# One transformer block on one core: w_ada laid out with a feature in each row, one multiply-and-sum a block on VectorE, and the first columns in four rounds of 2, 3, 5 and 6 blocks

## The chip, the core and the metric

The program runs on one core of a Trainium2 chip. The metric is the device time of one execution, in microseconds (us), from the start of the launch to its end; lower is better. The core's engines run side by side, each through its own list of instructions in a fixed order: TensorE (PE) multiplies matrices into PSUM, VectorE (DVE) and ScalarE (ACT) work element by element, SyncE (SP) issues nearly all transfers from HBM to SBUF, and GpSimd (POOL) does little here.

## The reference

One block over 256 tokens of width D = 2048, all in float32. What matters here is cut out of it:

```python
c_act = jax.nn.silu(c)                                  # (1, 2048)
mod = c_act @ w_ada[l] + b_ada[l]                       # w_ada (2048, 6 * 2048)
sh1, sc1, gt1, sh2, sc2, gt2 = jnp.split(mod, 6, axis=-1)
h = ada_norm(x, g_norm1[l], sh1, sc1)                   # rmsnorm(x, g) * (1 + sc1) + sh1
aq, ak, av, iq, ik, iw, hq, hf, hi, hog, ga, gh = split_cols(h @ w_in[l])
...
x = x + gt1[:, None] * (merged @ w_out[l])
h2 = ada_norm(x, g_norm2[l], sh2, sc2)
x = x + gt2[:, None] * hier_moe(h2, ...)                # 32 experts
return rmsnorm(x, g_final)
```

`mod` is a product of one vector with a matrix of 2048 x 12288: 100.7 MB that are read once. Each column of `h @ w_in` needs all 2048 features of h, and so all of sh1 and sc1; sc2, sh2, gt1 and gt2 are needed only from the product with w_out on.

## The kernel before, in words

A block is 128 features (KT = 16 blocks make 2048). Every product of the dense part (w_in, w_attn_up, w_hgrn_up, w_out) is taken as three float32r products: ACT rounds a weight tile to its high part (`split_w`, line 254), DVE subtracts for the low part (line 255), and PE runs high x high, high x low, low x high (`three`, lines 276 to 278) for each of the two halves t of the tokens. A pair of weight blocks against 512 columns is thus one ACT instruction and one DVE instruction of 128x1024 and 12 matmuls.

Weights come through `unit` (line 206): a ring of four SBUF tiles of up to 1 MB, filled by SP in the program's order. A tile is loaded anew when the engine that reads it last is done with it.

**First columns.** While w_ada is still being read, `first_columns` already works on 9 chunks of w_in's columns (seven of 512, two of 292) in rounds over blocks of features. FIRST_GROUPS gives each round its first block and its number of blocks: (0, 2), (2, 2), (4, 4), (8, 4), (12, 4). A round needs sc1 and sh1 of its own blocks only. At its start h of these blocks is made (lines 510 to 524); then, chunk by chunk, the weights are split, multiplied, and the PSUM results copied out by ACT (first round) or added by DVE onto the sums so far (line 543, two adds a chunk). Behind each chunk stands a unit of w_ada for the next round (`ada_block`). From the fifth chunk of the last round on, steps of attention and of the recurrence are taken in between.

**The vector times w_ada.** In HBM w_ada is packed with input features as partitions. In the first rounds a unit is 1 MB and PE multiplies it by a zero-padded 128x32 tile of c (line 494); for sh1 of rounds 2 and 3 (FIRST_DVE, counted from 0) DVE does it instead, with one multiply-and-add of 128x512 for each input block (line 489). The partial sums lie over partitions or in rows, so `ada_columns` (line 398) turns them into columns with small PE products. The other 64 units (`next_ada`) are taken one behind each unit of a later product, with each sixth call left out: the first 8 by PE (line 422), the other 56 by DVE, four instructions of 128x512 each (line 427). The gates gt1 and gt2 stay as partial sums over the partitions, with the bias in one row, and `gate_rows` sums them with a matrix of ones.

**The rest.** `middle_columns` (names hcol, hog, gate), `merge` (up) and `project` (out) follow. Last come the 32 experts: 384 tiles of 1 MB of weights are loaded and multiplied, in an order written by hand. Outside the experts the order on each engine is set by a scheduler from the program's dependencies and its written order.

Of the kernel before, what the change touches and what calls it, by code (L numbers as in the profile page):

```python
# [29 lines left out]
FIRST_GROUPS = ((0, 2), (2, 2), (4, 4), (8, 4), (12, 4))  # L30
FIRST_DVE = (2, 3)
# [57 lines left out]

def _blocks():  # L90


    for j0, nk in FIRST_GROUPS:
        ku = KT // nk
        for q in range(nk):
            for part in (1, 0):
                yield "w_ada", ku * q, ku, part * D + 128 * j0, 128 * nk
        for c0, n in FIRST_COLS:
            yield "w_in", j0, nk, c0, n
    for c0 in range(2 * D, 6 * D, 512):  # L100
        for q in range(4):
            yield "w_ada", 4 * q, 4, c0, 512
# [18 lines left out]
def packed(arrays):  # L121
# [14 lines left out]
class Block:  # L136
# [27 lines left out]
    def t2(self, shape, dt=F32, tag="t2"):  # L164
        return self.dn.tile(shape, dt, name=self.name("t2"), tag=tag, bufs=25)
# [115 lines left out]
    def prepare(self):  # L281
# [5 lines left out]
        crow = self.dn.tile([16, 128], F32, name="crow")  # L287
        nc.sync.dma_start(crow, a["c"].rearrange("o (r f) -> (o r) f", f=128))
# [24 lines left out]
        ps = self.misc()  # L313
        nc.tensor.transpose(ps[:, :16], crow, self.ident[:16, :16])
        th = self.sm([128, 32])
        nc.scalar.activation(th[:, :16], ps[:, :16], AF.Tanh, scale=0.5)
        ca = self.keepd([128, 16])
        nc.vector.scalar_tensor_tensor(ca, th[:, :16], 1.0, ps[:, :16], op0=OP.add, op1=OP.mult)
        nc.vector.tensor_scalar(ca, ca, 0.5, None, op0=OP.mult)
        self.ca = ca  # L320
        self.mod = {n: self.keep([128, 16]) for n in ("sc2", "sh2")}
        self.gates_in = {}
        self.ada_i, self.ada_call, self.ada_acc = 0, 0, [None, None]
        cpad = self.keepd([128, 16, 32])
        nc.gpsimd.memset(cpad, 0.0)
        nc.vector.tensor_copy(cpad[:, :, 0], ca)
        self.cpad = cpad
# [65 lines left out]
    def ada_columns(self, part, rhs):  # L393

        n, m = rhs.shape[-1], part.shape[-1] // 128
        ps = self.misc()
        for i in range(m):
            self.nc.tensor.matmul(ps[:, n * i:n * i + n], part[:, i * 128:(i + 1) * 128], rhs, start=True, stop=True)
        return ps[:, 0:m * n].rearrange("p (i r) -> p i r", r=n)

    def next_ada(self):

        self.ada_call += 1
        if self.ada_i == 64 or self.ada_call % ADA_SKIP == 0:
# [7 lines left out]
        c0 = 128 * base + 512 * c
        w = self.unit(("w_ada", 4 * q, c0, 512))
        if b > 7 and q == 0 and b not in self.gates_in:
            self.gate_room(b)
        if q == 0:
            self.ada_acc[on_dve] = self.gates_in[b] if b > 7 else self.t2([128, 512]) if on_dve else self.adabank()
        acc = self.ada_acc[on_dve]
        for i in range(4):
            j = 4 * q + i  # L420
            if not on_dve:
                nc.tensor.matmul(acc[32 * i:32 * i + 32, :], self.cpad[:, j, :], w[:, i, :], start=q == 0, stop=q == 3,
                                 skip_group_check=True)
            elif j == 0 and b < 8:
                nc.vector.tensor_scalar(acc, w[:, i, :], self.ca[:, j:j + 1], None, op0=OP.mult)
            else:
                nc.vector.scalar_tensor_tensor(acc, w[:, i, :], self.ca[:, j:j + 1], acc, op0=OP.mult, op1=OP.add)
        if q == 1 and 7 < b + 1 < 16:
            self.gate_room(b + 1)
        if q == 3 and b < 8:  # L430
            if not on_dve:
                ps, acc = acc, self.t2([128, 512])
                nc.scalar.activation(acc, ps, AF.Copy)
            v = self.ada_columns(acc, self.ones[:, 0:1])[:, :, 0]
            f = slice(4 * c, 4 * c + 4)
            add = self.bsc[:, 16:32] if name == "sc2" else self.cols[:, base:base + 16]
            nc.vector.tensor_add(self.mod[name][:, f], v, add[:, f])

    def gate_room(self, b):

        t = self.t2([128, 512])
        self.nc.gpsimd.memset(t, 0.0)
        c0 = (32 * 128, 80 * 128)[b // 12] + 512 * (b % 4)
        self.nc.gpsimd.dma_start(t[0:1, :], self.a["b_ada"][:, c0:c0 + 512])
        self.gates_in[b] = t

    def gate_rows(self, b, out):

        ps = self.misc()
        self.nc.tensor.matmul(ps, self.ones, self.gates_in[b], start=True, stop=True)  # L450
        self.nc.scalar.activation(out, ps, AF.Copy)


    def first_columns(self):
# [11 lines left out]
        bank = {}  # L466
# [4 lines left out]
        def ada_block(g, u):  # L471

            if g > last:
                return
            j0, nk = groups[g]
            ku = 16 // nk
            if u == 0:
                bank[g] = self.adabank(), self.t2([128, 512]) if g in FIRST_DVE else None
            ps, acc = bank[g]
            q, b = divmod(u, 2)  # L480
            if q * ku >= KT:
                return
            c0 = (D, 0)[b] + 128 * j0
            w = self.unit(("w_ada", ku * q, c0, 128 * nk))
            for i in range(ku):
                j = ku * q + i
                if b and acc is not None:
                    if j:
                        nc.vector.scalar_tensor_tensor(acc, w[:, i, :], self.ca[:, j:j + 1], acc, op0=OP.mult, op1=OP.add)
                    else:  # L490
                        nc.vector.tensor_scalar(acc, w[:, i, :], self.ca[:, j:j + 1], None, op0=OP.mult)
                    continue
                r = 64 * b + 32 * (i % 2)
                nc.tensor.matmul(ps[r:r + 32, 0:128 * nk], self.cpad[:, j, :], w[:, i, :], start=j < 2, stop=j >= KT - 2,
                                 skip_group_check=True)

        for u in range(8):
            ada_block(0, u)
        self.first_norm()
        for g, (j0, nk) in enumerate(groups):  # L500
# [6 lines left out]
            ps, acc = bank[g]  # L507
            rows = 128 if acc is None else 64
            part = self.t2([128, 512])
            nc.scalar.activation(part[:rows, 0:128 * nk], ps[:rows, 0:128 * nk], AF.Copy)  # L510
            v = self.ada_columns(part[:rows, 0:128 * nk], self.half[:rows])
            w = v[:, :, 1:2] if acc is None else self.ada_columns(acc, self.ones[:, 0:1])
            f = slice(j0, j0 + nk)
            G = self.sm([128, nk, 2])
            nc.vector.tensor_add(G[:, :, 0], v[:, :, 0], self.bsc[:, f])
            nc.vector.tensor_mul(G[:, :, 0], G[:, :, 0], self.cols[:, 96 + j0:96 + j0 + nk])
            nc.vector.tensor_add(G[:, :, 1], w[:, :, 0], self.cols[:, f])
            for i in range(nk):
                j = j0 + i
                h = self.t1([128, 256])  # L520
# [909 lines left out]
```

## Time and profile before

| | us |
|---|---|
| median of 3 runs | 1835.61 (1833.42 to 1838.31) |
| the profiled execution | 1836.52 |
| its span, first to last instruction | 1834.8 |
| PE busy | 1713.7 (93%) |
| DVE busy | 903.0 (49%) |
| ACT busy | 505.5 (28%) |

PE's busy time counts matmuls with modelled ends, which overlap: a stretch in which PE is busy all the time is one in which it had work, and the distance from one matmul's start to the next tells what a matmul costs. The shares are averages over stages with different limits, so the stages are read apart.

### The profile page before, as it was taken

How to read it: one execution, taken by the hardware profiler on the slowest of the kernel's cores; microseconds unless marked ns; L12 is line 12 of the kernel's file. 1: busy time of each engine (PE TensorE's matmuls, PEld its weight loads, DVE VectorE, ACT ScalarE, POOL GpSimd, SP SyncE). 2: the span in 40 equal slices, each digit the busy share in tenths (PEclk: the TensorE clock that was granted, in tenths of full speed). 3: DMA queues.
4: the chain of work that ended last, by engine and by line, in shares of the span. 5: the costliest groups of instructions: out<-in, count | busy, mean ns of one | idle time of the engine just before them, and what ended most of it. 6: DMA issues, size and time to landing. Idle time of an engine off the chain costs nothing. (4 is left out here: it accounts for less than half of the span.)

```text
span 1834.8 us, 20408 instructions
## 1 busy us (share of the span) xinstructions
PE 1713.7 (93%) x7925; PEld 992.0 (54%) x7925; DVE 903.0 (49%) x1636; ACT 505.5 (28%) x845; POOL 17.2 (1%) x36
## 2 busy tenths in 40 slices
PE   7899999999999999997999998998989989989895
PEld 4566676677778877774443443433434434334232
DVE  3677479698778899974122321232123221222125
ACT  3333244555554433443220020110201102002003
POOL 0000000000000000000000000000000000000000
PEclk9999999999999999997999999999999999999997
DMA  7887745776668888976999999999999999999995
GB/s 284 292 286 282 288 158 205 250 293 250 230 232 327 335 310 318 348 261 265 379 422 421 421 421 422 421 421 421 421 422 421 421 421 422 421 421 421 422 377 192
DMA packets 96485, 630.39 MB, mean 344 GB/s; under 512 B 14864, under 2 KB 17216, under 8 KB 22016
## 3 DMA queue, kind: packets, MB, share of 16 engines
q1 hardware_dynamic: 95008, 626.01, 86.1%
q0 software_dynamic: 1200, 2.96, 0.6%
q8 instruction: 64, 1.05, 0.2%
q14 instruction: 37, 0.30, 0.0%
q10 hardware_dynamic: 176, 0.07, 0.0%
HBM read 626.90 MB, written 2.10 MB: 343 GB/s over the span
## 5 line engine op out<-in xcount | busy, mean ns | idle before, releaser
L1160 PE MATMUL moe_acc<-moe_u,moe_xg 128*64 128x512 f32 x2048 | 487.6, 600 | 42.1 <-DMA moe_u<-w_exp_up 42.1
L1160 PEld LDWEIGHTS moe_acc<-moe_u,moe_xg 128*64 128x64 f32 x2048 | 157.3, 137 | 319.1 <-issue 219.0
L1267 PE MATMUL moe_acc<-moe_u,moe_hT 128*64 128x512 f32 (+1 forms) x1040 | 242.1, 590 | 10.9 <-DMA moe_u<-w_exp_down 10.9
L1219 DVE COPY moe_gu<-moe_acc 128x512 f32<-128x512 f32 x32 | 22.1, 691 | 355.5 <-PE moe_acc L1160 355.5
L1267 PEld LDWEIGHTS moe_acc<-moe_u,moe_hT 128*64 128x64 f32 x1040 | 88.3, 137 | 145.9 <-issue 109.5
L1270 DVE SCALAR_TENSOR_TENSOR moe_ys<-moe_acc,moe_cw,out_t 128x512 f32<-128x512 f32 (+1 forms) x65 | 48.3, 742 | 180.7 <-PE moe_acc L1267 180.6
L1272 ACT ACTIVATE moe_yp<-moe_ys 128x512 fp32r<-128x512 f32 (+1 forms) x65 | 40.5, 623 | 310.4 <-DVE moe_ys L1270 310.4
L276 PE MATMUL gate_acc<-gate_wr,first_t 128*128 128x512 f32 x256 | 103.3, 404 | 0.0
L277 PE MATMUL gate_acc<-gate_wl,first_t 128*128 128x512 f32 x256 | 102.2, 399 | 0.0
L278 PE MATMUL gate_acc<-gate_wr,first_t 128*128 128x512 f32 x256 | 101.8, 398 | 0.0
L1352 DVE TENSOR_TENSOR out_t<-out_t,moe_ps 128x512 f32<-128x512 f32 (+1 forms) x130 | 82.0, 672 | 35.6 <-PE moe_ps L1351 35.6
L1341 ACT ACTIVATE moe_xg<-moe_ps,pre_c,pre_c 128x256 f32<-128x256 f32 (+1 forms) x144 | 70.5, 539 | 80.9 <-PE moe_ps L1338 79.9
L254 ACT ACTIVATE gate_wr<-gate_u 128x1024 fp32r<-128x1024 f32 x64 | 67.8, 1059 | 85.9 <-PE gate_acc L278 80.7
L1230 ACT ACTIVATE moe_si<-moe_ps 128x256 f32<-128x256 f32 x32 | 12.2, 381 | 280.4 <-PE moe_ps L1227 280.4
L255 DVE TENSOR_TENSOR gate_wl<-gate_u,gate_wr 128x1024 fp32r<-128x1024 f32 x64 | 78.0, 1222 | 23.0 <-ACT gate_wr L254 22.8
L1338 PE MATMUL moe_ps<-moe_P,out_t 128*128 128x256 f32 (+1 forms) x576 | 82.2, 292 | 3.5 <-ACT moe_Sw L1256 2.8
L1338 PEld LDWEIGHTS moe_ps<-moe_P,out_t 128*128 128x128 f32 x576 | 72.7, 194 | 22.0 <-issue 16.1
L276 PE MATMUL lb_acc<-lb_wr,first_t 128*128 128x512 f32 (+1 forms) x208 | 79.3, 386 | 3.2 <-ACT first_t L523 2.4
L277 PE MATMUL lb_acc<-lb_wl,first_t 128*128 128x512 f32 (+1 forms) x208 | 79.1, 380 | 2.7 <-DVE lb_wl L255 2.7
L1351 PE MATMUL moe_ps<-moe_yp,moe_S 128*128 128x512 f32 (+1 forms) x260 | 78.4, 422 | 2.6 <-ACT moe_yp L1272 2.3
L278 PE MATMUL lb_acc<-lb_wr,first_t 128*128 128x512 f32 (+1 forms) x208 | 78.4, 378 | 0.0
L1351 PEld LDWEIGHTS moe_ps<-moe_yp,moe_S 128*128 128x128 f32 x260 | 44.0, 189 | 60.3 <-issue 49.9
(436 smaller groups left out, 2507.1 us busy)
## 6 DMA issues: line engine op xcount, KB each, us to landing
moe_u<-w_exp_gate SPq DMA_DIRECT2D x128, 1024.0 KB, 19.8
moe_u<-w_exp_up SPq DMA_DIRECT2D x128, 1024.0 KB, 19.8
moe_u<-w_exp_down SPq DMA_DIRECT2D x126, 1024.0 KB, 19.8
gate_u<-w_in SPq DMA_DIRECT2D x32, 1024.0 KB, 4.9
gate_u<-w_ada SPq DMA_DIRECT2D x26, 1024.0 KB, 5.6
lb_u<-w_in SPq DMA_DIRECT2D x20, 1024.0 KB, 6.0
first_u<-w_ada SPq DMA_DIRECT2D x17, 1024.0 KB, 6.7
out_u<-w_out SPq DMA_DIRECT2D x16, 1024.0 KB, 7.6
```

The source lines that it names most:

```text
L254: nc.scalar.activation(hi, raw, AF.Copy)
L255: nc.vector.tensor_sub(lo, raw, hi.bitcast(F32))
L276: mm(out, lr, hi, start=start, stop=False)
L277: mm(out, lr, lo, start=False, stop=False)
L278: mm(out, ll, hi, start=False, stop=stop)
L1160: nc.tensor.matmul(gu[e][64 * k:64 * k + 64, :], xg[g][j][:, CAP * i:CAP * i + CAP], w[k][:, jj, :], start=j == 0, stop=j == KT - 1, skip_ ...
L1267: nc.tensor.matmul(yp[64 * i:64 * i + 64, :n], h[i][:, f, :], w[i][:, f, :], start=f == 0, stop=f == 3, skip_group_check=True)
L1270: nc.vector.scalar_tensor_tensor(raw, yp[:, :n], cw, self.gt2[:, c0:c0 + n], op0=OP.mult, op1=OP.mult)
L1338: nc.tensor.matmul(ps[:, 0:n], self.xs[t][i][:, j * 128:(j + 1) * 128], P[t], start=t == 0 and i == 0, stop=t == 1 and i == 1)
L1341: nc.scalar.activation(x, ps[:, 0:n], AF.Identity, scale=self.mod["sc2"][:, j:j + 1], bias=self.mod["sh2"][:, j:j + 1])
L1351: self.nc.tensor.matmul(ps[:, :n], sc[:, t * 128:(t + 1) * 128], ys[i], start=i == 0, stop=i == 1)
L1352: self.nc.vector.tensor_add(self.z[t][:, s], self.z[t][:, s], ps[:, :n])
```

## The change

- `w_ada` is transposed in HBM: a row is an output feature, with its 2048 inputs. A block of 128 features is one tile of 128x2048 (1 MB, as before). `ada` loads it and takes it by one VectorE instruction, `tensor_tensor_reduce`: multiply by c, broadcast over the partitions, and sum along the row into one column of `mod`.
- c is loaded broadcast to 128 partitions (128x2048) at the head of SP's queue, and silu is one ACT instruction.
- PE has no w_ada product any more, `ada_columns` and the gates' rows go; `gate_rows` makes four diagonal tiles on ACT and sums these with the matrix of ones.
- The first columns run in four rounds of 2, 3, 5 and 6 blocks. A round's w_in tiles have at most 4 blocks (`pieces`), so the rounds of 5 and 6 load two a chunk; an odd block is split by instructions of half the width. h of a round is made before the last chunk of the round ahead of it; the scaling of h moves from DVE to ACT.
- The 512-wide SBUF buffers are 22 instead of 25; PSUM has one more buffer for small results.

```diff
-FIRST_GROUPS = ((0, 2), (2, 2), (4, 4), (8, 4), (12, 4))
-FIRST_DVE = (2, 3)
+FIRST_GROUPS = ((0, 2), (2, 3), (5, 5), (10, 6))
...
+SH1, SC1, GT1, SH2, SC2, GT2 = range(6)
+ADA_ORDER = [(part, j) for part in (SC2, SH2, GT1, GT2) for j in range(KT)]
...
+def pieces(j0, nk):
+
+    n = -(-nk // 4)
+    for i in range(n):
+        a, b = nk * i // n, nk * (i + 1) // n
+        yield j0 + a, b - a
...
+    out["w_ada"] = np.ascontiguousarray(arrays["w_ada"][0].T)
...
-        nc.sync.dma_start(crow, a["c"].rearrange("o (r f) -> (o r) f", f=128))
+        self.ca = self.keepd([128, D])
+        nc.sync.dma_start(self.ca, a["c"].to_broadcast([128, D]))
...
+        nc.scalar.activation(self.ca, self.ca, AF.Silu)
...
+    def ada(self, part, j):
+
+        w = self.big.tile([128, D], F32, name=self.name("u"), tag="ring", bufs=4)
+        r = 128 * (KT * part + j)
+        self.nc.sync.dma_start(w, self.a["w_ada"][r:r + 128, :])
+        self.nc.vector.tensor_tensor_reduce(w, w, self.ca, 1.0, 0.0, OP.mult, OP.add, self.mod[part][:, j:j + 1])
+
+    def next_ada(self):
+
+        self.ada_call += 1
+        if self.ada_i < len(ADA_ORDER) and self.ada_call % ADA_SKIP:
+            self.ada(*ADA_ORDER[self.ada_i])
+            self.ada_i += 1
...
+        todo = [[(part, j) for j in range(j0, j0 + nk) for part in (SC1, SH1)] for j0, nk in groups] + [[]]
...
+            ahead = todo[g + 1]
             for c, (c0, n) in enumerate(cols):
+                if c == len(cols) - 1 and g < last:
+                    features(g + 1)
                 acc = [self.acc(), self.acc()]
-                raw = self.unit(("w_in", j0, c0, n))
...
+                for u0, m in pieces(j0, nk):
+                    raw = self.unit(("w_in", u0, c0, n))
+                    for q in range(0, m, 2):
+                        hi, lo = self.split_w(raw[:, q:min(q + 2, m), :], n)
...
-                for u in range(8):
-                    if min(u, len(cols) - 1) == c:
-                        ada_block(g + 1, u)
+                k = len(cols) - 1
+                for block in ahead[len(ahead) * c // k:len(ahead) * (c + 1) // k]:
+                    self.ada(*block)
```

The scheduler's order shows where the work stands now. First VectorE, in the second round of the first columns, before: `first_acc` and `first_t` are the sums of line 543, `first_u ... pre_d` a w_ada tile times c, `first_wl` the low part of a weight tile.

```order
L489 SCALAR_TENSOR_TENSOR first_t_550<-first_u_579,pre_d_91,first_t_550 128x512 x2
L255 TENSOR_TENSOR first_wl_590<-first_u_587,first_wr_589 128x1024
L543 TENSOR_TENSOR first_t_277<-first_t_277,first_acc_527 128x512
L543 TENSOR_TENSOR first_t_279<-first_t_279,first_acc_528 128x512
L489 SCALAR_TENSOR_TENSOR first_t_550<-first_u_579,pre_d_91,first_t_550 128x512
```

The same engine and round in the changed kernel; the multiply-and-sum (`ISA`, line 382) has a second row of 128x1 that writes out its sum.

```order
L382 ISA first_u_531,pre_d_88<-first_u_531,pre_d_69 128x2048
L382 ISA pre_d_88 128x1
L471 TENSOR_TENSOR first_t_262<-first_t_262,first_acc_499 128x512
L471 TENSOR_TENSOR first_t_264<-first_t_264,first_acc_500 128x512
L251 TENSOR_TENSOR first_wl_539<-first_u_536,first_wr_538 128x1024
L251 TENSOR_TENSOR first_wl_555<-first_u_536,first_wr_554 128x512
L382 ISA first_u_566,pre_d_89<-first_u_566,pre_d_69 128x2048
L382 ISA pre_d_89 128x1
```

Every w_ada tile of the round now stands in VectorE's list, between the splits and the adds that PE waits for, and a split of three blocks takes two instructions.

PE in the second round before, between two chunks of columns: `first_ada` is the product of a w_ada tile with the padded c.

```order
L277 MATMUL first_acc_586<-first_wl_590,first_t_106 128x512
L278 MATMUL first_acc_586<-first_wr_589,first_t_108 128x512
L494 MATMUL first_ada_549<-first_u_607,pre_d_96 32x512 x4
L276 MATMUL first_acc_613<-first_wr_617,first_t_106 128x292
L277 MATMUL first_acc_613<-first_wl_618,first_t_106 128x292
```

PE between two chunks of the same round in the changed kernel:

```order
L273 MATMUL first_acc_500<-first_wl_520,first_t_101 128x512
L274 MATMUL first_acc_500<-first_wr_519,first_t_103 128x512
L272 MATMUL first_acc_534<-first_wr_538,first_t_101 128x512
L272 MATMUL first_acc_535<-first_wr_538,first_t_101 128x512
L273 MATMUL first_acc_534<-first_wl_539,first_t_101 128x512
```

The w_ada products are gone from PE's list; nothing takes their place.

## Rows read from the trace of the kernel before

**Rows 1.** The page: span, and busy time of PE.
```profile
span 1834.8 us, 20408 instructions
PE 1713.7 (93%) x7925; PEld 992.0 (54%) x7925; DVE 903.0 (49%) x1636; ACT 505.5 (28%) x845; POOL 17.2 (1%) x36
```

**Rows 2.** Windows by stage: length, engines' busy time, PE clock, DMA share, GB/s.
```profile
0.00:32.00 32.00, 19.10 (x148) 13.19 (x148) 11.82 (x42) 8.54 (x20) 2.65 (x8) 1.00 0.83 311
32.00:66.00 34.00, 31.98 (x168) 21.95 (x168) 13.48 (x19) 19.08 (x31) 0.00 (x0) 1.00 0.79 265
66.00:108.00 42.00, 37.56 (x162) 22.80 (x159) 32.61 (x52) 10.03 (x12) 0.00 (x0) 0.96 0.80 272
108.00:169.00 61.00, 57.13 (x265) 41.24 (x265) 46.43 (x75) 20.59 (x26) 0.00 (x0) 1.00 0.85 322
169.00:233.00 64.00, 62.04 (x286) 41.31 (x282) 34.36 (x50) 19.52 (x24) 0.00 (x0) 1.00 0.70 259
233.00:289.00 56.00, 54.62 (x251) 43.04 (x252) 44.34 (x100) 26.95 (x45) 0.00 (x0) 0.94 0.46 161
289.00:355.00 66.00, 65.54 (x303) 43.26 (x301) 51.86 (x131) 31.63 (x57) 0.54 (x1) 1.00 0.61 220
355.00:411.00 56.00, 56.00 (x260) 43.88 (x261) 48.77 (x76) 29.58 (x53) 0.54 (x1) 1.00 0.80 296
411.00:636.00 225.00, 224.69 (x1077) 178.39 (x1076) 185.32 (x310) 111.67 (x165) 8.71 (x17) 1.00 0.74 274
636.00:733.00 97.00, 94.06 (x412) 74.70 (x412) 90.62 (x113) 37.51 (x40) 2.67 (x5) 1.00 0.84 312
733.00:845.00 112.00, 109.23 (x507) 86.09 (x505) 84.34 (x117) 44.38 (x61) 2.15 (x4) 0.99 0.77 283
845.00:1835.00 990.00, 901.72 (x4100) 382.12 (x4100) 259.02 (x565) 146.01 (x316) 0.00 (x0) 0.98 0.98 404
```

**Rows 3.** Groups of DVE instructions by shape, first 860 us: count, busy us, mean ns.
```profile
L255 DVE TENSOR_TENSOR gate_wl<-gate_u,gate_wr 128x1024 fp32r<-128x1024 f32 x64 | 78.0, 1222 | 23.0 <-ACT gate_wr L254 22.8
L427 DVE SCALAR_TENSOR_TENSOR gate_t<-gate_u,pre_d,gate_t 128x512 f32<-128x512 f32 x92 | 68.8, 747 | 2.4 <-DMA gate_u<-w_ada 1.1
L543 DVE TENSOR_TENSOR first_t<-first_t,lb_acc 128x512 f32<-128x512 f32 x40 | 26.7, 683 | 16.5 <-PE lb_acc L278 16.3
L679 DVE SCALAR_TENSOR_TENSOR att_t<-att_t,att_sm,att_t 128x256 f32<-128x256 f32 x7 | 3.4, 482 | 0.4
L524 DVE TENSOR_TENSOR first_t<-first_t,first_t 128x256 fp32r<-128x256 f32 x8 | 3.0, 417 | 0.2 <-ACT first_t L523 0.2
```

**Rows 4.** Windows of lines 494, 422 and 398 alone: PE and PEld busy time.
```profile
sum 845.00, PE 50.15 PEld 14.02; mean PE 7.16 PEld 2.00
...
289.00:845.00 556.00, 10.61 (x64) 1.52 (x64) 1.00 0.75 278
...
289.00:845.00 556.00, 7.59 (x64) 8.39 (x64) 1.00 0.75 278
```

**Rows 5.** Timeline of PE where the first round begins: start, us, instruction.
```profile
32.80 0.51 PE L276 MATMUL first_acc<-first_wr,first_t 128*128 128x512 f32 x1 [0.59 <-ACT first_t L523]
...
33.60 0.39 PE L276 MATMUL first_acc<-first_wr,first_t 128*128 128x512 f32 x1
33.83 0.40 PE L277 MATMUL first_acc<-first_wl,first_t 128*128 128x512 f32 x1
```

**Rows 6.** SP's waits (32 to 169), and transfers (32 to 289): KB, us to landing.
```profile
SPq L206 <- PE first_ada L494: 32.6, 10, 5.8
...
first_u<-w_ada SPq DMA_DIRECT2D x11, 1024.0 KB, 6.0
first_u<-w_in SPq DMA_DIRECT2D x11, 512.0 KB, 5.4
```

**Rows 7.** Windows of PE in the second round: busy time and granted clock.
```profile
88.00:92.00 4.00, 1.56 (x7) 1.00 0.98 302
92.00:96.00 4.00, 4.00 (x13) 0.57 0.90 281
```

More of the change, by code (lines that the diff above doesn't have):

```diff
@@ L87, in constants @@
     return k
+def pieces(j0, nk):
[3 more added lines that the diff above has]
+        yield j0 + a, b - a
 def _blocks():
     for j0, nk in FIRST_GROUPS:
[L94 to L97, printed above, removed]
         for c0, n in FIRST_COLS:
[L99 to L102, printed above, removed]
+            for j, m in pieces(j0, nk):
+                yield "w_in", j, m, c0, n
     taken = {c0 for c0, _ in FIRST_COLS}
@@ L312, in prepare @@
         self.ones = ones
[L313 to L327, printed above, removed]
+        nc.scalar.activation(self.ca, self.ca, AF.Silu)
+        self.mod = [self.keep([128, 16]) if part in (SH2, SC2) else self.keepd([128, 16]) for part in range(6)]
+        self.ada_i, self.ada_call = 0, 0
         cols = self.keep([128, 128])
@@ L412, in next_ada @@
[L412 to L418, printed above, removed]
-        for i in range(4):
[L420 to L447, printed above, removed]
+        f = slice(4 * b, 4 * b + 4)
+        col = self.sm([128, 4])
+        nc.vector.tensor_add(col, self.mod[part][:, f], self.cols[:, KT * part:KT * part + KT][:, f])
+        dg = self.t2([128, 512])
@@ L465, in first_columns, with features @@
         self.v = [[None] * 2 for _ in range(2)]
-        bank = {}
         groups = FIRST_GROUPS
         last = len(groups) - 1
-        def ada_block(g, u):
-            if g > last:
-                return
+        def features(g):
             j0, nk = groups[g]
[L476 to L495, printed above, removed]
-        for u in range(8):
-            ada_block(0, u)
+            f = slice(j0, j0 + nk)
+            G = self.sm([128, nk, 2])
+            nc.vector.tensor_add(G[:, :, 0], self.mod[SC1][:, f], self.bsc[:, f])
+            nc.vector.tensor_mul(G[:, :, 0], G[:, :, 0], self.cols[:, 96 + j0:96 + j0 + nk])
+            nc.vector.tensor_add(G[:, :, 1], self.mod[SH1][:, f], self.cols[:, f])
+            for i in range(nk):
+                j = j0 + i
+                h = self.t1([128, 256])
+                hr, hl = self.hr[j // 8][:, j % 8, :], self.hl[j // 8][:, j % 8, :]
+                nc.scalar.activation(h, self.yT[j // 8][:, j % 8, :], AF.Identity, scale=G[:, i, 0:1], bias=G[:, i, 1:2])
+                nc.scalar.activation(hr, h, AF.Copy)
+                nc.vector.tensor_sub(hl, h, hr.bitcast(F32))
+        todo = [[(part, j) for j in range(j0, j0 + nk) for part in (SC1, SH1)] for j0, nk in groups] + [[]]
+        for block in todo[0]:
+            self.ada(*block)
         self.first_norm()
+        features(0)
         for g, (j0, nk) in enumerate(groups):
@@ L545, in first_columns @@
                             self.gate2(z[t][c], z[t][c], self.t2([128, 512]))
-                for u in range(8):
-                    if min(u, len(cols) - 1) == c:
-                        ada_block(g + 1, u)
+                k = len(cols) - 1
+                for block in ahead[len(ahead) * c // k:len(ahead) * (c + 1) // k]:
+                    self.ada(*block)
                 if g == last and c > 4:
```

73 lines of the change are left out of this document (18 added, 55 removed).

## The prediction

> **What bounds the kernel now.** I read the page first: PE is busy 93% of the span [rows 1]. That is a mean, so I cut the span into windows, one for each round of the first columns and one for each later product [rows 2]. The last window, the experts from 845 on, moves 404 GB/s at a DMA share of 0.98. It is bound by its weights, holds no w_ada, and starts when the dense part has let go of its buffers; so every microsecond that the dense part gains or loses passes to the end. From 289 to 845 PE is busy nearly throughout: 549.5 of 556 us in five windows. DVE is close behind in some of them, 51.9 of 66, 48.8 of 56, 185.3 of 225 and 90.6 of 97 us. From 32 to 289 no single engine binds: PE is busy 32.0 of 34, 37.6 of 42, 57.1 of 61, 62.0 of 64 and 54.6 of 56 us in the five rounds, and DVE 13.5, 32.6, 46.4, 34.4 and 44.3.
>
> In the rounds the ring of four tiles counts as well. The first takes 9 w_in tiles and 4 of w_ada in 34 us, the second 9 and 8 in 42: 2.6 and 2.5 us a tile. A tile of 512 KB takes 5.4 us to land and one of 1024 KB takes 6.0 [rows 6], so a small tile holds its place nearly as long as a full one. SP waited 32.6 us for PE's w_ada products to free tiles [rows 6], since these stand in PE's list behind the products of the chunk.
>
> **What PE loses.** The w_ada products of line 494 keep PE busy 50.2 us, all before 289; line 422 has 10.6 us and the column products of line 398 have 7.6 us behind 289 [rows 4]. What stays: matmuls of 512 columns start every 0.235 us (33.60 to 33.83) [rows 5]. A block takes 6 of them a chunk, and two of the nine chunks have 292 columns, about 0.134 us by columns. That is 6 x (7 x 0.235 + 2 x 0.134) = 11.5 us a block. Rounds of 2, 3, 5 and 6 blocks need 23, 35, 57 and 69 us. The last round also holds attention's products: before, it took 54.6 us busy with 4 blocks, 46 by this count, so 8 more; it needs 77 us.
>
> **What VectorE gets.** No instruction of 128x2048 with a sum stands in the trace. The nearest rows multiply and add with two operands in SBUF: 482 ns at 256 elements and 747 ns at 512 [rows 3], so 1.035 ns an element and 217 ns fixed. At 2048 that gives 2.34 us. The second row, which writes out the sum, costs between nothing and another 0.22 us; I take 0.16, so 2.5 us a block. The upper bound is half the pace, if summing while reading two operands took two steps an element: 0.22 + 2048 x 2.07 = 4.46, with the second row 4.6 us.
>
> [...] No run here shows the form with a sum.
>
> For a block that DVE took before, four instructions of 0.747 us (2.99) become 2.5. For a block that PE took, 2.5 us are new. By round, from the rows' durations (a split of 1024 takes 1.22, half of it or an add 0.68, of 292 columns about 0.45, of 584 about 0.77; 0.42 for each low part of h):
> - Round of 2: splits 10.1, 6 w_ada blocks 15, low parts 1.3: 26 us.
> - Round of 3: splits 15.8 (a full and a half one a chunk), adds 11.4, 10 blocks 25, low parts 2: 54 us.
> - Round of 5: splits 25.8, adds 11.4, 12 blocks 30, low parts and lower bounds 5: 72 us.
> - Round of 6: splits 31.5, adds 11.4, the rest as before about 15: 58 us.
>
> **The rounds' new lengths.** The largest need decides, and beside it the ring at 2.5 us a tile: 15, 19, 30 and 18 tiles, so 37, 48, 75 and 45 us. DVE frees a w_ada tile as soon as it has read it, so the ring should do better than before in the first round. There I take 34 us (needs 23 PE, 26 DVE, at most 37 ring). The round of 3 is DVE's, 54 plus 2 for waits. The round of 5 has DVE 72 and ring 75; I take 77. The round of 6 is PE's, 77 plus 1. The start: the first product begins at 32.8 [rows 5]. One more transfer of 1.05 MB stands ahead of all others (at most 3.4 us at the 311 GB/s of the first window [rows 2]), and four blocks on DVE take the place of PE's products in the same chain; I take 1 us later, out of 0 to 4. Sum: 33.8 + 34 + 56 + 77 + 78 = 279 against 289: 10 us gained. Bounds: if the bare needs hold, 33 + 27 + 54 + 73 + 77 = 264, 25 gained; with 2.6 us a tile, 15% of waits on DVE and dips of PE's clock, about 307, 18 lost.
>
> **Behind 289.** The 64 later blocks stand 7, 7, 26, 14 and 10 in the five windows.
> - 289 to 355: all 7 were PE's. PE falls by 9.3 + 1; DVE rises by 17.5 to 69 of 66 us. It becomes the bound: 3 us lost.
> - 355 to 411: PE falls by 1.3 + 1.9, DVE stays at 48: 3 gained.
> - 411 to 636: five column products of 0.95 go from a full PE; DVE falls by 26 x 0.49 to 173: 4.7 gained.
> - 636 to 733: DVE falls from 90.6 to 84, and PE's 2.9 us of waits shrink: 2 gained.
> - 733 to 845: nothing goes from PE; the gates' four small ACT copies hide beside an ACT that is busy 44 of 112 us (uncovered, a few us): 0.
>
> That is 7 us gained, with bounds 20 (everything PE loses, and the waits) and 0. The scaling of h on ACT is hidden, since ACT is busy at most 19.1 of 34 us in a round [rows 2]; if it weren't, it would delay the start of a round, which is why its being put ahead of the last chunk matters. I cost the fewer buffers at nothing, as the gates' partial sums no longer hold eight of them; without that cover, wider instructions would wait for one another in the out stage.
>
> **Sum.** 10 + 7 = 17 us off the profiled execution's 1836.5, which stands 0.9 above the median: 1819.
>
> **The rivals.**
> 1. *The needs hold bare*: DVE and PE run through their rounds without gaps, and DVE's surplus in 289 to 355 is taken up later. 25 + 20 = 45 gained: 1791. For it: SP no longer waits for PE. Against it: every round of before stood 2 to 4 us above PE's busy time, and the second had a ring and PE both short of full.
> 2. *Nothing to be seen*: what PE gives up in the rounds is paid back by DVE and the ring: 40 us of PE become 53 us of waiting for DVE. Both parts together within 5 us: about 1834.
> 3. *Half pace of the multiply-and-sum*: 4.6 us a block. [...] The start and the rounds of 2, 3 and 5 gain 8, 13, 21 and 25 us, so DVE needs 39, 75 and 97, and the dense part reaches 289's place 41 us late; behind it 289 to 355 takes 84, 355 to 411 takes 63, 411 to 636 about 230, 636 to 733 takes 113: 46 more. About 1924. About 50 of the 96 blocks lie where DVE binds, so the kernel is slower than before from some 2.9 us a block.
> 4. *The list in order*: DVE waits for a w_ada tile that has not landed, and the split behind it, and so PE, wait too. [...] By the bound above 18 lost in the rounds, 3 gained behind: 1851. It decides from about 12% of waits on DVE.
>
> **Chances.** The forecast of 17 gained (6 to 38) 0.48; rival 1 0.18; rival 2 0.14; rival 4 0.13; rival 3 0.07. A measurement of this kernel tells about 0.3%, 5.5 us, from no change. So faster 0.66, same 0.14, slower 0.20. The forecast's own range is 1798 to 1831; to hold 8 in 10 it must reach rival 1 and most of rival 4: 1788 to 1848.
>
> **What would show it.** The multiply-and-sum's group: 2.3 to 2.4 us and a short second row. DVE busy over 90% of the rounds of 3 and 5, with PE at two thirds and waiting for the low part (line 251). The product named hcol begins near 279 and lasts as long as before, the one named gate about 5 us less. The experts' stretch keeps its 990 us. The prediction is wrong if the multiply-and-sum takes 3 us or more, if the round of 3 ends much under 50 us, or if the experts' stretch changes.

## The result, and the profile after

The changed kernel takes 1818.51 us (median of 4 runs, 1815.76 to 1820.87) against 1835.02 of the kernel before: a ratio of 0.9907, 95% interval 0.9884 to 0.9930. That is 16.5 us faster; 17 were forecast. The sum came out. Some of its terms did not, so that it came out this closely is in part luck. The experiments show that the new grouping of the rounds gives back more than half of what the rest of the change gains.

The profiled execution took 1820.87 us. Its page, beside [rows 1]:

```profile
span 1819.1 us, 19433 instructions
PE 1653.9 (91%) x7492; PEld 987.9 (54%) x7492; DVE 922.8 (51%) x1552; ACT 524.6 (29%) x905; POOL 8.5 (0%) x19
```

PE lost 60 us of busy time, DVE gained 20. Now the windows by stage, with the columns of [rows 2]: the start, the four rounds (cut where the last sum of a round is added), hcol, hog, gate, up, out, and what follows.

```profile
0.00:36.00 36.00, 10.33 (x65) 10.07 (x66) 19.04 (x45) 12.65 (x25) 2.12 (x7) 1.00 0.83 319
36.00:73.00 37.00, 28.43 (x108) 21.40 (x107) 24.20 (x29) 17.93 (x31) 0.00 (x0) 0.86 0.80 271
73.00:129.00 56.00, 42.97 (x170) 32.93 (x169) 51.39 (x69) 20.35 (x34) 0.00 (x0) 0.88 0.84 305
129.00:211.00 82.00, 65.61 (x273) 50.72 (x272) 68.76 (x107) 29.74 (x45) 0.00 (x0) 0.92 0.80 287
211.00:285.40 74.40, 73.31 (x361) 59.66 (x360) 55.87 (x109) 35.87 (x57) 0.00 (x0) 1.00 0.57 194
285.40:352.30 66.90, 59.89 (x241) 44.73 (x240) 61.73 (x128) 29.98 (x55) 0.54 (x1) 0.92 0.59 218
352.30:407.10 54.80, 53.38 (x238) 41.94 (x236) 48.78 (x65) 29.17 (x51) 0.54 (x1) 1.00 0.84 308
407.10:628.10 221.00, 220.26 (x1039) 174.00 (x1038) 174.20 (x257) 112.44 (x167) 2.07 (x4) 1.00 0.76 279
628.10:721.10 93.00, 92.32 (x410) 74.56 (x409) 81.65 (x85) 38.79 (x44) 1.08 (x2) 1.00 0.90 332
721.10:825.00 103.90, 103.45 (x478) 83.01 (x477) 72.18 (x81) 49.10 (x81) 2.16 (x4) 1.00 0.77 285
825.00:1819.00 994.00, 903.95 (x4130) 394.89 (x4128) 264.99 (x586) 148.54 (x323) 0.00 (x0) 0.98 0.98 404
```

Read the second and third columns (PE, DVE) of the rounds against each other. In the last round PE is busy 73.3 of 74.4 us and DVE has 18 us to spare. In the three rounds ahead of it PE is busy 137 of 175 us, DVE 144, and neither is full; PE's mean granted clock is 0.86 to 0.92 there, against 1.00 in the last round. In the trace of before, hcol began at 288.8 and the last product of out started at 836.6; now they stand at 285.4 and 824.5. So 3.4 us come from the part up to hcol and 8.7 from the products behind it. The other 3.6 between the two profiled executions stand in the experts' part, whose products are the same in both. From the last matmul of out to the end it took 997.8 us in the one profile of before, 994.1 in this one, and 992.5 to 996.3 in the twelve profiles of the experiments. One profile of before doesn't tell whether these 3.6 us belong to the change or to the execution.

The multiply-and-sum by shape on DVE (instructions, busy us, mean ns of one), here the 21 whose tile is named first_u, and its second row in 64 blocks, the last line:

```profile
L382 DVE CUSTOM_DVE_ANT_0 first_u<-first_u,pre_d 128x2048 f32<-128x2048 f32 x21 | 48.0, 2288 | 3.8 <-DMA first_u<-w_ada 3.8
L382 DVE DVE_READ_ACCUMULATOR2_ANT pre_d<- 128x1 f32 x64 | 5.4, 85 | 0.0
```

2.29 + 0.08 = 2.37 us a block. The line through the two-operand rows [rows 3] gave 2.34 for the first instruction, and half its pace would have been 4.5 us.

The rows of that line, 747 ns at 512 elements and 482 at 256, read two tiles. Two rows of before that read one tile stand beside them:

```profile
L425 DVE TENSOR_SCALAR gate_t<-gate_u,pre_d 128x512 f32<-128x512 f32 x4 | 1.9, 479 | 0.0
...
L677 DVE TENSOR_SCALAR att_t<-att_t,att_sm 128x256 f32<-128x256 f32 x1 | 0.3, 343 | 0.0
```

That is 0.53 ns an element with one tile read, 343 to 479 ns from 256 to 512 elements, against 1.035 with two. So whatever makes the two-tile rows the slower ones is in the line to 2.34 us already, and the 2.29 us measured rule out only a further halving by the sum. That the second tile is what costs isn't shown, since the two instructions differ in other ways too.

### The profile page after: what moved, and what is told of

The parts are those of the page before. It is cut to its first block, busy times and chain, and to the rows that moved or that the text cites. A ratio compares the mean times of both kernels' runs of the same rounds, so it can differ in the third digit from the quotient of the medians.

```text
span 1819.1 us, 19433 instructions
## 1 busy us (share of the span) xinstructions
PE 1653.9 (91%) x7492; PEld 987.9 (54%) x7492; DVE 922.8 (51%) x1552; ACT 524.6 (29%) x905; POOL 8.5 (0%) x19
## 5 line engine op out<-in xcount | busy, mean ns | idle before, releaser
L1090 PEld LDWEIGHTS moe_acc<-moe_u,moe_xg 128*64 128x64 f32 x2048 | 164.7, 137 | 315.5 <-issue 208.4
L1197 PE MATMUL moe_acc<-moe_u,moe_hT 128*64 128x512 f32 (+1 forms) x1040 | 242.8, 590 | 10.4 <-DMA moe_u<-w_exp_down 10.4
L1271 ACT ACTIVATE moe_xg<-moe_ps,pre_c,pre_c 128x256 f32<-128x256 f32 (+1 forms) x144 | 69.6, 543 | 79.2 <-PE moe_ps L1268 78.5
L273 PE MATMUL lb_acc<-lb_wl,first_t 128*128 128x512 f32 (+1 forms) x188 | 72.9, 388 | 14.1 <-DVE lb_wl L251 14.1
L272 PE MATMUL lb_acc<-lb_wr,first_t 128*128 128x512 f32 (+1 forms) x188 | 71.2, 387 | 2.3 <-ACT lb_wr L250 2.1
L274 PE MATMUL lb_acc<-lb_wr,first_t 128*128 128x512 f32 (+1 forms) x188 | 72.1, 384 | 0.0
```

What stands on the lines that cost most here:

```text
L272: mm(out, lr, hi, start=start, stop=False)
L273: mm(out, lr, lo, start=False, stop=False)
L274: mm(out, ll, hi, start=False, stop=stop)
L1090: nc.tensor.matmul(gu[e][64 * k:64 * k + 64, :], xg[g][j][:, CAP * i:CAP * i + CAP], w[k][:, jj, :], start=j == 0, stop=j == KT - 1, skip_ ...
L1197: nc.tensor.matmul(yp[64 * i:64 * i + 64, :n], h[i][:, f, :], w[i][:, f, :], start=f == 0, stop=f == 3, skip_group_check=True)
L1271: nc.scalar.activation(x, ps[:, 0:n], AF.Identity, scale=self.mod[SC2][:, j:j + 1], bias=self.mod[SH2][:, j:j + 1])
```

## The experiments

| kernel | median, us | ratio to before | 95% interval |
|---|---|---|---|
| changed | 1818.51 | 0.9907 | 0.9884 to 0.9930 |
| e1 old rounds 2, 2, 4, 4, 4 | 1797.70 | 0.9807 | 0.9783 to 0.9830 |
| e2 sums doubled in the rounds | 1855.58 | 1.0119 | 1.0092 to 1.0147 |
| e3 sums doubled behind them | 1887.10 | 1.0296 | 1.0269 to 1.0322 |
| e4 sums of 256 in the rounds | 1806.83 | 0.9856 | 0.9833 to 0.9880 |
| e5 start in order | 1815.89 | 0.9897 | 0.9881 to 0.9913 |
| e6 e1 with small tiles | 1804.68 | 0.9837 | 0.9820 to 0.9855 |
| e7 rounds 2, 4, 4, 6 | 1817.16 | 0.9897 | 0.9880 to 0.9915 |
| e8 sums a chunk earlier | 1824.62 | 0.9940 | 0.9926 to 0.9953 |
| e9 w_ada blocks in the last round | 1818.95 | 0.9912 | 0.9894 to 0.9930 |
| e10 rounds 2, 4, 6, 4 | 1806.77 | 0.9837 | 0.9816 to 0.9859 |
| e11 e1 with e5's start | 1800.65 | 0.9807 | 0.9787 to 0.9826 |
| e12 e11 with e9's idea | 1801.88 | 0.9823 | 0.9803 to 0.9844 |

**e1, the old rounds.**

```diff
-FIRST_GROUPS = ((0, 2), (2, 3), (5, 5), (10, 6))
+FIRST_GROUPS = ((0, 2), (2, 2), (4, 4), (8, 4), (12, 4))
```

> The changed kernel with the old rounds of 2, 2, 4, 4, 4 blocks: the layout and the multiply-and-sum alone. Theory (the layout brings the gain, the grouping a little): by the needs of my prediction with the measured 2.37 us a block, the rounds take 34, 45, 58, 58 and 59 us behind a first product at 36, so the product named hcol begins near 290 instead of 285.4, and the kernel takes about 1823 us. Rival (the grouping brings it: one round less saves 18 adds of 0.68 us on a VectorE that binds): 12 us lost, 1831 us.

Measured: 1797.70, 20.8 us faster than the changed kernel. Both accounts expected it to be slower. Windows of its rounds and of hcol:

```profile
36.70:63.00 26.30, 24.41 (x111) 18.62 (x109) 19.92 (x26) 17.27 (x30) 0.00 (x0) 1.00 0.89 298
63.00:107.00 44.00, 30.20 (x108) 21.11 (x108) 38.70 (x51) 12.63 (x19) 0.00 (x0) 0.88 0.85 299
107.00:163.00 56.00, 49.28 (x224) 38.70 (x225) 53.61 (x71) 23.59 (x32) 0.00 (x0) 1.00 0.88 326
163.00:215.00 52.00, 46.96 (x216) 37.25 (x215) 48.82 (x64) 20.05 (x26) 0.00 (x0) 1.00 0.87 323
215.00:266.80 51.80, 50.98 (x250) 40.57 (x249) 44.52 (x89) 26.34 (x40) 0.00 (x0) 1.00 0.56 191
266.80:328.20 61.40, 55.37 (x230) 41.64 (x228) 59.33 (x134) 27.95 (x48) 0.00 (x0) 0.97 0.68 246
```

Compare sums, not single rounds. All rounds but the last take 178 us here for 12 blocks of w_in beside 28 of w_ada; in the changed kernel they took 175 for 10 beside the same 28 (and 171 in e3 and e9, whose code is the same up to the last round). DVE is busy 161 of the 178 us, against 144 of 175. The last round is PE's in both: 4 blocks in 52 us, 6 in 74. So two blocks moved ahead of the last round cost 3 to 7 us there and save 22 at PE's pace. hcol is 5.5 us shorter too, with 11 matmuls fewer in it; hog has as many more and is 0.7 us longer.

**e7 and e10, the order of rounds.** Both have four rounds, and the same numbers of blocks. The edit of e7; in e10 the last two pairs are (6, 6) and (12, 4):

```diff
-FIRST_GROUPS = ((0, 2), (2, 3), (5, 5), (10, 6))
+FIRST_GROUPS = ((0, 2), (2, 4), (6, 4), (10, 6))
```

> The changed kernel with four rounds of 2, 4, 4, 6 blocks instead of 2, 3, 5, 6: the same last round, and the same TensorE work (115 us) and w_ada blocks (28) ahead of it, but 9 w_in tiles in each of the first three rounds instead of 9, 9 and 18, and no split of half the width there. Theory (the tiles of 2 and 3 blocks of the round of 5 cost the ring's places): 55 tiles at 2.6 us are 143 behind a first product at 36, the last round 82, so hcol begins at 261 to 268 and the kernel takes 1793 to 1800 us. Rival (the long last round without w_ada is the cause, since it leaves 28 blocks to 115 us of TensorE where the old rounds leave them to 138): hcol at 280 to 285, 1813 to 1818 us.

> The changed kernel with four rounds of 2, 4, 6, 4 blocks: those of the run with 2, 4, 4, 6, with the round of 6 ahead of that of 4; w_ada blocks 8, 12 and 8 beside them. Theory (the 28 blocks and the w_in tiles beside them take VectorE and the ring some 175 to 183 us in any grouping, and the last round lies behind them at TensorE's pace, so that fewer blocks in it are better): last round 52 us, hcol at 263 to 271, 1795 to 1803 us. Rival 1 (four rounds, with their larger h to make at a time, are worse than five as such): hcol at 279 or later, 1815 us and more. Rival 2 (the 18 small tiles of the round of 6 take the ring 2.7 us each): first three rounds 195 us, hcol at 283, 1819 us.

Measured: 1817.16, as the rival of e7 had it, and 1806.77, between the theory of e10 and its two rivals. The rounds of e7, then those of e10 and its hcol:

```profile
34.30:81.00 46.70, 33.28 (x110) 23.12 (x108) 31.61 (x37) 19.39 (x34) 0.00 (x0) 0.78 0.82 289
81.00:137.00 56.00, 50.42 (x223) 39.88 (x223) 49.43 (x63) 24.83 (x33) 0.00 (x0) 0.97 0.80 298
137.00:205.00 68.00, 53.27 (x218) 41.43 (x217) 61.14 (x91) 22.22 (x33) 0.00 (x0) 0.90 0.83 302
205.00:279.00 74.00, 72.94 (x359) 59.31 (x358) 56.61 (x116) 36.08 (x57) 0.00 (x0) 1.00 0.57 194
```

```profile
35.40:82.00 46.60, 33.28 (x110) 22.97 (x109) 31.41 (x36) 18.55 (x34) 0.00 (x0) 0.78 0.82 290
82.00:153.00 71.00, 57.16 (x226) 44.12 (x227) 60.69 (x75) 26.59 (x37) 0.00 (x0) 0.90 0.79 291
153.00:225.00 72.00, 69.60 (x321) 56.91 (x320) 60.91 (x98) 31.19 (x44) 0.00 (x0) 0.98 0.82 296
225.00:276.90 51.90, 51.08 (x250) 40.67 (x249) 43.39 (x79) 25.93 (x40) 0.00 (x0) 1.00 0.52 187
276.90:338.40 61.50, 55.48 (x229) 41.46 (x227) 59.35 (x134) 27.90 (x48) 0.00 (x0) 0.97 0.69 246
```

e7 has nine w_in tiles fewer ahead of its last round than the changed kernel, and no split of half the width in it, and gains nothing: 171 us up to its last round, then 74. So odd blocks and small tiles are not what costs the 21 us. Moving the round of 6 ahead (e10) makes the last round 52 us, as forecast, but the first three 190 instead of the 175 to 183 expected; rival 2 had said 195. Its own mechanism, the small tiles of the round of 6, isn't seen: that round is PE's, busy 69.6 of 72 us, and 118 us went into the two rounds ahead of it. e10 gains 10.4 us on e7; in the profiles hcol begins 2 us earlier and is itself 5.4 us shorter (in e7 it takes from 279.0 to 345.9). So a short last round is better, as the theory says, but here the two blocks moved ahead cost 19 of the 22 us that they save, and most of the gain lies in hcol, which the theory didn't name. e1 does the same blocks and as many tiles ahead of its last round in 178 us instead of 190, so how the w_ada blocks are spread over the rounds counts as well.

**e6, the ring.** The rounds of e1, with

```diff
-    n = -(-nk // 4)
+    n = -(-nk // 2)
```

> The old rounds of 2, 2, 4, 4, 4 blocks as in the first experiment, with each w_in tile of 4 blocks (1 MB) loaded as two tiles of 2 blocks (512 KB): the same bytes and the same instructions on VectorE, ScalarE and TensorE, but 18 more tiles through the ring of four in the third and fourth round (and 9 in the last, where the ring has time to spare). Theory (tiles count: a tile holds its place about 2.6 us whatever its size): 18 x 1 to 2.6 us longer, 1816 to 1845 us. Rival (VectorE alone binds these rounds): under 4 us, 1797 to 1802 us.

Measured: 7.0 us slower than e1 for 18 tiles more ahead of the last round, 0.4 us a tile, with intervals that just touch. Neither account's number: tiles count a little, and not 2.6 us each. The rounds of 4 became 59 us each.

**e2 and e4, VectorE's time in the rounds.** In `ada`, for the 28 blocks taken in the first three rounds: in e2 a second `tensor_tensor_reduce` into a scratch column, and in e4 a shorter one:

```diff
-        self.nc.vector.tensor_tensor_reduce(w, w, self.ca, 1.0, 0.0, OP.mult, OP.add, self.mod[part][:, j:j + 1])
+        n = 256 if part in (SC1, SH1) and j > 1 else D
+        self.nc.vector.tensor_tensor_reduce(w[:, :n], w[:, :n], self.ca[:, :n], 1.0, 0.0, OP.mult, OP.add,
+                                            self.mod[part][:, j:j + 1])
```

> The multiply-and-sum of the 28 blocks taken within the first three rounds is done twice, the second time into a scratch column: 28 x 2.37 = 66 us more on VectorE, nothing else. Theory (VectorE binds the rounds of 3 and 5): VectorE needs 36 us in the round of 2, 71 in the round of 3 and 94 in the round of 5; with the waits of today 4, 21 and 21 us longer, so 46 in all, about 1865 us. Rival (the ring of four tiles binds as well and hides part of it, or the time lies in waits that VectorE's list has anyway): under 25 us longer, below 1844 us.

> In the 28 blocks taken within the first three rounds the multiply-and-sum takes only 256 of the 2048 inputs, so most of sc1 and sh1 is left out; transfers, ring and all else stay. VectorE loses 28 x 1.9 = 52 us. Theory (VectorE binds the rounds of 3 and 5, the ring of four tiles stands close behind at 2.5 us a tile): the round of 3 falls from 51 to 48 and that of 5 from 79 to 75, or somewhat less where tiles are freed sooner: 7 to 12 us faster, about 1809 us. Rival 1 (VectorE alone binds): the rounds fall to TensorE's 38 and 63 us, 25 to 28 us faster, about 1792. Rival 2 (ring and list order bind, not VectorE): no change, 1818.

Measured: 37.1 us slower and 11.7 us faster. The first three rounds of e2, and then of e4:

```profile
35.60:72.00 36.40, 28.89 (x111) 22.03 (x109) 36.12 (x39) 16.97 (x27) 0.00 (x0) 0.86 0.83 268
72.00:150.00 78.00, 50.41 (x171) 39.14 (x171) 74.56 (x91) 22.29 (x37) 0.00 (x0) 0.76 0.66 237
150.00:247.00 97.00, 67.67 (x269) 53.83 (x268) 91.79 (x128) 28.98 (x42) 0.00 (x0) 0.82 0.67 235
```

```profile
35.00:69.00 34.00, 26.02 (x110) 19.23 (x109) 15.67 (x34) 18.79 (x33) 0.00 (x0) 0.95 0.81 302
69.00:122.00 53.00, 40.00 (x165) 30.81 (x165) 32.70 (x69) 20.75 (x33) 0.00 (x0) 0.90 0.86 313
122.00:199.00 77.00, 65.29 (x276) 50.63 (x276) 45.60 (x102) 28.49 (x42) 0.00 (x0) 0.93 0.81 309
```

Three points of one curve: with DVE busy 94, 144 and 202 us the three rounds take 164, 175 and 211. Only in the last is DVE full (96%). From 144 down to 94 each us taken from DVE gives back 0.2 us: something else holds the rounds at 164, at 2.6 us for each of the 64 tiles, with DVE busy 57% of the time and PE 80%. So VectorE alone is not what binds the changed kernel's rounds, though it is close. Both edits also change how long a w_ada tile holds its place in the ring, by 2.4 us more in e2 and 1.9 less in e4, so the curve doesn't separate VectorE's time from the ring's. And the middle point moves: the same code took 171 us in the profiles of e3 and e9.

**e3, VectorE's time behind the first columns.** The second sum for the 64 later blocks.

> The multiply-and-sum of the 64 blocks taken behind the first columns is done twice: 152 us more on VectorE. Theory (VectorE stands close behind TensorE in the products named hcol, hog, gate and up): their VectorE needs become 78, 66, 236 and 115 us where they now take 67, 55, 221 and 93, and out 101 of 104, so 65 to 75 us longer, about 1888 us. By this one would pay about half of what VectorE gets more. Rival (covered by TensorE): under 25 us longer, below 1844 us.

Measured: 68.6 us slower, within the 65 to 75 of the theory: 0.45 us for each of the 152 us added. hcol, up and out of this run (the last product of out starts at 887.0):

```profile
279.00:354.70 75.70, 61.47 (x243) 45.18 (x242) 75.14 (x142) 30.68 (x57) 0.54 (x1) 0.89 0.54 198
652.30:764.10 111.80, 99.42 (x410) 76.76 (x408) 110.00 (x112) 37.75 (x41) 1.06 (x2) 0.95 0.76 277
764.10:890.00 125.90, 114.59 (x497) 88.61 (x495) 104.93 (x127) 53.37 (x90) 2.15 (x4) 0.96 0.70 254
```

DVE is now busy 99% and 98% in hcol and up, where it was 92% and 88%. The total fits, its parts less so: out was to stay at 104 us and takes 123, 19 of the 68.6 us, with DVE not full there.

**e5 and e11, the start.** With copies of the normed x by `nc.scalar.activation(..., AF.Copy)` and, in `first_columns`, where `first_norm` now returns its `r`,

```diff
+        r = self.first_norm()
+        for part in (SC1, SH1):
+            nc.vector.tensor_scalar(self.mod[part][:, 0:2], r, 0.0, None, op0=OP.mult)
         for block in todo[0]:
             self.ada(*block)
-        self.first_norm()
```

The two `tensor_scalar` write zeros into the columns that the first sums overwrite, so that these sums must wait for `r`, the end of the norm's chain.

> The changed kernel with its start put in order: the four multiply-and-sums of the first round wait until the chain of small instructions of the first norm is through, and the eight copies of the normed x stand on ScalarE instead of VectorE. The chain then ends at 19.7 us instead of 26.1, the four sums at 29.7, the first product begins at 32 instead of 36.0. Theory (the start's 3.2 us lost pass to the end): 4 us faster, about 1814.5 us. Rival (the ring binds the round of 2: the first tiles come free 3 us later than now, and the round ends at 70 as before): no change, 1818 us.

> The old rounds of 2, 2, 4, 4, 4 with the start put in order as in the start experiment (there the first product came 4.5 us earlier and 2.6 us were left at the end). Theory (in the round of 2 with only 4 w_ada blocks beside it TensorE is busy 23.8 of 25.6 us, so the ring doesn't swallow it): 4 to 5 us faster than with the old rounds alone, about 1793 us. Rival (later rounds are VectorE's and the ring's, and swallow part of it as there): 0 to 2.6 us, 1795 to 1798 us.

This is the timeline of DVE in the changed kernel which they undo (start us, us):

```profile
16.94 0.17 DVE L232 TENSOR_SCALAR first_sm<-first_sm 128x2 f32<-128x2 f32 x1
17.02 2.28 DVE L382 CUSTOM_DVE_ANT_0 first_u<-first_u,pre_d 128x2048 f32<-128x2048 f32 x1
19.23 0.08 DVE L382 DVE_READ_ACCUMULATOR2_ANT pre_d<- 128x1 f32 x1
19.23 0.16 DVE L211 TENSOR_SCALAR first_sm<-first_sm 128x2 int32<-128x2 int32 x1
```

A sum of 2.3 us stands between two links of the norm's chain, whose next link is 0.16 us long; three such stand in the chain, and PE's products on the normed x begin at 26.1, against 19.2 in e5. Measured: the first product comes at 31.5 and 32.0 instead of 36.0 and 36.7. In e5 the median is 2.6 us lower, with intervals that overlap, which lies between the theory and the rival and doesn't decide between them: in its profile hcol begins at 280.9 instead of 285.4, so all of the earlier start is still there, though its round of 5 took 85 us instead of 82. In e11 nothing is left (ratio 0.9807 both): hcol begins at 269.8 instead of 266.8, and its third round took 62 us instead of 56,

```profile
103.00:165.00 62.00, 51.85 (x221) 40.05 (x222) 53.50 (x72) 23.05 (x31) 0.00 (x0) 0.94 0.80 300
```

with DVE as busy in us as in e1, and the mean clock 0.94 instead of 1.00. So in e11 the rival holds. It isn't settled why that round stretched; its instructions stood in another order, too.

**e8, the boundary between rounds.**

```diff
-                k = len(cols) - 1
-                for block in ahead[len(ahead) * c // k:len(ahead) * (c + 1) // k]:
+                k = len(cols) - 2
+                for block in ahead[len(ahead) * min(c, k) // k:len(ahead) * min(c + 1, k) // k]:
```

> The changed kernel with a round's w_ada blocks spread over its chunks but the last two, instead of all but the last; so the last sums of a round come a chunk earlier and h of the next round with them. Theory (the wait of 3.6 us at the start of the last round, behind a multiply-and-sum that stands ahead of a split in VectorE's list, and the fall of the clock behind it make the last round 85 us instead of 78): 5 to 7 us faster, about 1812 us. Rival (VectorE is full ahead of the boundary, so the wait only moves into an earlier chunk): no change, 1818 us.

Here is the wait meant, on PE of the changed kernel (in brackets: idle before, and what ended it), with windows of 4 us around it:

```profile
200.58 0.79 PE L273 MATMUL lb_acc<-lb_wl,first_t 128*128 128x512 f32 x1 [3.63 <-DVE lb_wl L251]
```

```profile
196.90:200.90 4.00, 0.37 (x2) 0.32 (x2) 3.67 (x6) 1.48 (x4) 0.00 (x0) 0.78 0.62 224
200.90:204.90 4.00, 4.00 (x10) 2.81 (x9) 3.09 (x12) 4.00 (x10) 0.00 (x0) 0.50 0.85 289
```

PE stood nearly still for 4 us, and in the next 4 the granted clock was 0.50; in windows of 0.2 us it is 0.50 up to 205.8 and 1.00 from 206.0 on. In e8 two such waits stand elsewhere and are as long:

```profile
181.57 0.50 PE L273 MATMUL lb_acc<-lb_wl,first_t 128*128 128x512 f32 x1 [3.66 <-DVE lb_wl L251]
...
192.37 0.50 PE L273 MATMUL lb_acc<-lb_wl,first_t 128*128 128x512 f32 x1 [3.56 <-DVE lb_wl L251]
```

Such a wait isn't always followed by a lower clock: in e8 the matmuls of 512 columns from 181.91 to 188 take 0.39 or 0.40 us each, as they do at a clock of 1.00 [rows 5], and behind the second wait the one at 193.74 takes 0.63 us, as those at 0.50 in the changed kernel do. Measured: 1824.62, some 6 us slower, with intervals that just touch. The wait moved, as the rival says. What cost the 6 us isn't shown: hcol begins at 286.2 in this profile, against 285.4 in that of the changed kernel. The expectation's placing was wrong as well: the wait lies in the last chunk of the round of 5, not in the last round, which ran at PE's pace without it.

**e9 and e12, VectorE's idle time in the last round.** `self.next_ada()` in the first five chunks of the last round (in e12 three, on top of e11).

> The changed kernel with five of the 64 later w_ada blocks taken in the first five chunks of the last round, where VectorE is busy 57 of 75 us and the ring moves half of what it could; all later blocks move up by five. Theory (the last round leaves VectorE idle, and VectorE is what hcol waits for, with 62 of 67 us busy): hcol and what follows lose 11.9 us of VectorE at the 0.45 us that the doubled sums behind the first columns cost for each, 5 us faster, about 1813 us. Rival (hcol waits for the chain of attention's steps, not for VectorE's time): no change, 1818 us, and if the splits of the last round are held up, slower.

> The same as the run beside it (old rounds, start in order), with three later w_ada blocks taken in the first three chunks of the last round, where VectorE is busy 45 of 52 us. Theory (hcol is VectorE's there too, 59 of 61 us): 7.1 us of VectorE at 0.45, 3 us faster than the run beside it, about 1790 us. Rival (the last round's splits are held up): no change or 1 to 2 us slower.

Measured: no change in both. Last round, hcol and hog of e9:

```profile
205.00:282.10 77.10, 73.52 (x358) 59.31 (x357) 66.44 (x127) 36.58 (x59) 0.00 (x0) 1.00 0.67 245
282.10:343.40 61.30, 56.76 (x240) 42.66 (x239) 60.21 (x127) 29.90 (x54) 0.54 (x1) 0.97 0.65 240
343.40:402.30 58.90, 55.14 (x237) 43.28 (x236) 49.40 (x66) 29.81 (x53) 0.54 (x1) 0.97 0.78 295
```

hcol is 5.6 us shorter, about as expected; the last round is 2.7 longer and hog 4.1. The gain was there and was given back on both sides, so my 0.45 us for each us of DVE, measured on work added, did not hold for work moved.

## Why the prediction was right, and where it was wrong

**Luck.** 10 us were forecast up to hcol and 7 behind it. In the profile 3.4 came up to hcol, 8.7 behind it, and 3.6 in the experts' part, where none was forecast. In e3, the same code up to hcol, 9.4 came there. So the sum gave the direction and the rough size, and that it met the median within 1 us is luck.

**The price of a block** was 2.5 us and is 2.37; right. Rival 3 falls with it. Its total can be estimated, if the price of an added us is the same all along: e2 and e3 add 2.37 us to 92 of the 96 blocks and cost 37.1 + 68.6 = 105.7 us, so 0.485 us for each us. That a sum halves the pace was rival 3's assumption, and no run shows it: the instruction took 2.29 us, not 4.46. Half pace, the 4.6 us of rival 3, would add 2.23 us to 96 blocks, so 104 us, 1922 against the 1924 given. The kernel would be no faster than before from 16.5 / (96 x 0.485) = 0.35 us more, 2.7 us a block; I said 2.9.

**The start** was sized at 1 us out of 0 to 4 and cost 3.2 in this profile; the ten profiles with the same start have their first product at 33.8 to 36.7, so 1.0 to 3.9. The transfer ahead was foreseen (x's first square starts at 10.9 instead of 8.2). That a sum would be put between the links of the norm's chain was not; the order showed it and I did not read it there.

**The rounds** were to take 34, 56, 77 and 78 us and took 37, 56, 82 and 74. The mis-sized term is the round of 5. Its DVE is busy 69 us as counted (72), but that is 84% and not over 90%, and PE is busy 80% and not two thirds, since it works 15% longer than its 57 us by count at a clock of 0.92. The round of 3 fits (DVE 92%). The last round was PE's, with less of attention in it than counted. SP's waits for PE's products [rows 6] are gone; between 36 and 211 it waits for DVE, but for 0.3 us for a transfer; here the two longest:

```profile
SPq L202 <- DVE pre_d L382: 36.4, 12, 5.2
SPq L202 <- DVE lb_wl L251: 24.1, 11, 6.4
```

and PE waits mostly for the low part, as said:

```profile
PE lb_acc L273 <- DVE lb_wl L251: 14.1, 8, 3.6
PE first_acc L273 <- DVE first_wl L251: 12.0, 10, 2.0
```

In sum 279 was forecast for hcol and 285.4 came. Part of that is this execution: in e3 the first product came 2.2 us earlier, the first three rounds took 171 us instead of 175, and hcol began at 279.4.

**Behind hcol's start** 7 us were forecast and 8.7 came: hcol 0 instead of 3 lost, hog 1 instead of 3 gained, gate 4 and up 3 (forecast 4.7 and 2), out 0. That PE is full in gate, up and out is seen in the windows; that DVE holds hcol is borne out by e3 (75.7 us with DVE busy 99%), though hcol's DVE was busy 62 us and not the 69 counted. The experts' part kept its length within 4 us.

**The step that failed** is one that I did not write out: I costed layout and grouping as one, by adding each round's largest need, and never asked what the rounds' sizes do with the layout alone. By e1 all of the change but the grouping (the layout, with h made earlier and its scaling on ACT) is worth 37 us (its 1797.70 against 1834.93), and the grouping takes 21 of them. My needs put e1's rounds at 34, 45, 58, 58 and 59 us, 254 in all; they took 26, 44, 56, 52 and 52, in all 230. What the runs show in its place: w_in blocks left for the last round cost 11 us each at PE's pace (74 us for 6 and 52 for 4, in the changed kernel against e1 and in e7 against e10), with no w_ada beside them and DVE and transfers partly idle, while two blocks moved ahead of it cost 3 to 7 us in e1 and 19 in e10. The first holds in both pairs; what sets the second is open. Rival 4's waits are there, and so is a lower clock, as in [rows 7] before (0.86 to 0.92 in three rounds), but no run isolates their price: with PE's mean clock at 0.89 these rounds took 175 us, and with 0.91 in e5, whose start differs, 174.5.

**What stays open.** What holds the three rounds at 164 us in e4, with neither engine full, isn't taken apart: tiles (0.4 us each by e6), lists in order and the clock may all be in it. The ring is a rival that was not varied. SP waits 147.5 us for DVE to free its tiles between 36 and 211 in the changed kernel, where DVE is busy 144 of 175 us; and these rounds move 289 to 314 GB/s in the changed kernel, e1, e4 to e7, e10 and e11, and 241 in e2, against 404 in the experts. A ring of more than four tiles was not tried, nor were the new rounds with the old layout. Why hcol is 5 us shorter behind a short last round is open too. No variant beat e1, which is the fastest version here, 37 us below the kernel before.

## What to carry to other kernels

Where a side job that streams its own weights runs beside rounds of matrix work, put little into the round that runs without it: rounds of 2, 2, 4, 4, 4 and of 2, 4, 6, 4 beat those that end with 6 here. Cost the parts of a change apart even when they come together, since the sum can be right while one part undoes another. Don't count a free engine's time in full: a us of VectorE added or taken was worth 0.2 to 0.6 us here, by where it lay, and nothing in the two runs that only moved it.

## What the hardware showed unexpectedly

Summing along 2048 elements with both operands in SBUF costs no more than the line through plain two-operand rows gives: 2286 ns against 2.34 us, and 84 ns for writing out the sum, half of the 150 to 170 ns that instructions of one or two elements a row take. Cutting 1 MB tiles into two of 512 KB costs 0.4 us for each of the 18 tiles added ahead of the last round (e6), although a tile of 512 KB took 5.4 us to land before and one of 1024 KB 6.0 [rows 6]. Executions of the same code differ early: the first sums of the second round start at 78.5 us in the profile of the changed kernel and at 72.4 in that of e9, whose code is the same up to there. So a few us between the rounds of two single profiles decide nothing; the medians do.
